# Rows of finished output units squared and scaled under the seventh unit, and the recurrence's additional turns gathered in one column group

## The chip, the cores and the metric

One core of a Trainium2 chip. The metric is the device time of one execution in microseconds, as the median of several runs; the kernel before took 1652.8 us (three runs, 1652.15 to 1653.36). Beside it stands one profiled execution, from which all rows of the profile come.

The engines are named as the profile names them: PE is TensorE (matmuls), PEld its weight loads, DVE is VectorE, ACT is ScalarE, POOL is GpSimd, SP is the engine whose queue issues most DMAs. Each engine works through its own instructions in the order that was fixed when the kernel was built.

## The reference

An encoder of two layers on a sequence of 512 rows with 2048 columns, all in float32. Layer 1 mixes grouped-query attention and a gated linear recurrence; layer 2 is a chunked mLSTM that runs forward and backward. Cut to what matters:

```python
# layer 1 (even)
proj = rmsnorm(x) @ w_in            # q, k, v, g_attn, x_lru, g_lru
attn = block_attention(rope(q), rope(k), v)                  # 8 heads, 2 key heads
xc = conv4(x_lru)
y = rg_lru(xc, ..., reverse=False) + rg_lru(xc, ..., reverse=True)
x = x + concat(attn * silu(g_attn), y * silu(g_lru)) @ w_out

# one direction of rg_lru: two gates, then a scan along the sequence
r = sigmoid(xb @ wa + ba); i = sigmoid(xb @ wx + bx)
a = exp(8 * r * log_sigmoid(lam)); u = sqrt(1 - a * a) * i * xc
h[t] = a[t] * h[t - 1] + u[t]

# layer 2 (odd)
q, k, v, o, z, gates = rmsnorm(x) @ w_in
h = mlstm(q, k, v, gates) + flip(mlstm(flip(q), ...))        # 8 heads
h = rmsnorm_per_head(sigmoid(o) * h) * silu(z)
x = x + h @ w_out

out = x * rsqrt(mean(x * x, axis=-1) + 1e-6) * final_gain
```

The last line matters most here: each row's factor needs the squares of all its 2048 columns.

## The kernel before, in words

**Layout.** The residual stream lies transposed: 128 columns of x on the partitions, 512 sequence rows along the free dimension. A pair of such column blocks is a unit of 256 columns: units 0 to 7 of the output. A weight product in float32 is made of three matmuls of rounded parts (high by high, low by high, high by low; `mm3`, L157), so every weight chunk is first split: ACT writes the high part (L153), DVE the rest (L154).

**Column groups and lanes.** `run_steps` works through a list of groups. An ordinary group makes 512 columns of a projection: eight steps c of a 256-deep weight chunk, in each four blocks b of six matmuls. The weights are loaded three steps ahead and split two steps ahead (`ahead`). Between the blocks other work is let in by turns: two lanes of Python generators, and `pump(lane)` runs the first generator of a lane up to its next `yield`. Lane 0 holds attention and, in layer 2, the heads; it gets a turn after block 1 of each step (`turns` names other blocks). Lane 1 holds the recurrent units of layer 1 and the transposes `hT_gen` of layer 2; it gets one turn at the end of each step, and additional ones where a group has `more`:

```python
if b == 1 and c % 8 < g.get("more", 0):
    self.pump(1)
```

In layer 1 the groups come in the order KV, Q0, L0, L1, Q1, GL0, GL1, GA0, GA1, and then four groups of the output product. L0 and L1 make the recurrence's input, and each adds two units `lru_gen` to lane 1. Such a unit has 13 turns: two convolutions with their splits (L862, L153, L154), four of gates (each six matmuls `lg` and two DVE additions, L880), one of sigmoid and tanh on ACT, one of exponentials and L912, one empty, one of square roots, one empty, and two of scans (L923, L925). The groups with `more=5` are Q1, GL0 and GL1. Lane 0 meanwhile does the first key head's attention up to Q1, the second one's q in GL0 and its attention from the end of GL0 to GA1. The output product's operands are made by `mix_split`, from step 0 of GA1 on; where a needed part isn't there, it draws the lanes dry. A finished part whose gate isn't there yet is stored to DRAM and loaded again (`value_ready`, `mix_load`).

In layer 2, `hT_gen` squares a head pair's result (L1183), works out the row factors, scales on ACT (L1194), and then transposes block by block on PE (`hT`).

**The output product.** Units 0 and 1 are one ordinary group; their rows are squared into the running sum `acc`, scaled, and stored to DRAM (`x3d`). Units 2 to 6 are made by seven products instead of eight (`run_w7`). Units 2 to 5 (`LATE`) are added in DRAM onto the residual `x2d` by an accumulating DMA from POOL's queue (`out2_onto`); unit 5's goes out in unit 6's fourth step. Unit 6 is added on the chip (`out2_7`, L1373), squared, scaled. During unit 6, a hook `each(c)` loads finished units back: 0, 1, 2, 3, 4 in steps 3 to 7; `run_last` loads what is missing, unit 5. All loads go by SP's queue, between the weight loads.

The slots that these rows need come from one pool of 37 (`NSLOT`), of which 32 hold the operands of the output product; unit 6 frees two a step.

**The last unit (`run_last`).** Unit 7 is made in three parts. `rows()` makes its columns for sequence rows 0 to 255; `columns(0)` and `columns(1)` make rows 256 to 383 and 384 to 511 with the roles of the operands exchanged. Ahead of them in the program stand the squares and scales of units 2 to 5: `late_square` for the halves h0 (sequence rows 0 to 255, sums on DVE) and h1 (256 to 511, sums on POOL), then `late_scale` for h0; `late_scale` for h1 comes after `rows()`. The addition of unit 7 (L1410) and its square (L1419) follow. The row sums `stc` (a matmul of `acc` and the last square with ones) are taken up at k = 1 of `columns(0)`; DVE works out the factors, PE spreads them (`rB`), and every row block is scaled (L1480) and stored.

**Order.** What each engine does in which order is planned at build time from program order and readiness: `high_priority` moves evacuations ahead, and an instruction that is planned to wait can be passed by later ones of the same engine. At run time nothing is passed.

Of the kernel before, what the change touches and what calls it, by code (L numbers as in the profile page):

```python
# [15 lines left out]
AF = mybir.ActivationFunctionType  # L16
ALU = mybir.AluOpType
# [15 lines left out]
LATE = (2, 3, 4, 5)  # L33
# [8 lines left out]
class Builder:  # L42
# [255 lines left out]
    def run_steps(self, groups):  # L298
        self.steps = [(g, c) for g in groups for c in range(NCH)]
        self.raw, self.wsp = {}, {}  # L300
        self.nload = self.nsplit = 0
        self.ahead(0, 2, 1)
        i = 0
        for g in groups:
            if g["lay"] == "W7":
                self.run_w7(g, i)
                i += NCH
                continue
            if g["lay"] == "W7c":
                self.run_w7c(g, i)  # L310
                i += NCH
                continue
            g["ps"] = [None] * 4
            while self.later:
                self.evac_later()
            if g["lay"] == "last":
                self.run_last(g, i)
                i += NCH
                continue
            for c in range(NCH):  # L320
                self.ahead(i, 3, 2)
                g["c"] = c
                ws = self.wsp.pop(i)
                for b in range(g.get("nb", 4)):
                    if c == 0:
                        g["ps"][b] = self.bank.tile([P, 512], F32, tag="bulk", name=self.name("bk"))
                    self.bulk_mm(g, g["ps"][b], g["x"](c), ws, b, c)
                    if (c < NCH - 1 or b < 1 and "turns" in g) and b in g.get("turns", (1,)):
                        self.pump(0)
                    if b == 1 and c % 8 < g.get("more", 0):  # L330
                        self.pump(1)
                    if c == NCH - 1 and b == 0 and g.get("mid"):
                        g["mid"]()
                if c == NCH - 1:
                    with self.tc.high_priority(offset=100):
                        for b in range(g.get("nb", 4)):
                            g["evac"](b, g["ps"][b])
                    if g.get("after"):
                        g["after"]()
                    self.pump(0)  # L340
                self.pump(1)
                i += 1
# [647 lines left out]
class Layer2(Layer1):  # L990
# [217 lines left out]
    def hT_gen(self, p):  # L1208
        nc = self.nc
        for hs in self.h_norm(p):  # L1210
            yield
        for c in (2 * p, 2 * p + 1):
            t = self.slot2("hT")
            if p < 3:
                z = [self.half("zt") for _ in range(2)]
                for j in range(2):
                    nc.sync.dma_start(out=z[j], in_=self.zTd[(2 * c + j) * P:(2 * c + j + 1) * P, :])
            for j in range(2):
                k = 2 * c + j
                f = slice((k - 4 * p) * P, (k - 4 * p + 1) * P)  # L1220
                ps = self.psum("hT")
                for tt in range(NT):
                    self.tr(ps[:, tt * P:(tt + 1) * P], hs[tt // 2][:, tt % 2, f], self.ident)
                gn = self.pb[:, PB_GN + k:PB_GN + k + 1]
                nc.scalar.activation(t[:, j, :], ps, AF.Copy, scale=gn)
                if p < 3:
                    nc.gpsimd.tensor_tensor(out=t[:, j, :], in0=t[:, j, :], in1=z[j], op=ALU.mult)
                yield
            if p == 3:
                self.h3[c] = t  # L1230
                continue
            nc.sync.dma_start(out=self.hTd[2 * c * P:(2 * c + 2) * P, :].rearrange("(j p) s -> p j s", p=P), in_=t)
            self.hT_stored.add(c)
# [148 lines left out]
        self.xres[i] = self.slot2("xres")  # L1382
        self.nc.sync.dma_start(out=self.xres[i], in_=self.x3d[i] if i in self.x3d else self.rows2(self.x2d, i))

    def late_square(self, i, cs):

        sq = self.half("sq3").rearrange("p (j s) -> p j s", j=2)
        self.nc.scalar.activation(sq, self.xres[i][:, :, cs], AF.Square)
        eng = self.nc.gpsimd if cs.start else self.nc.vector
        for j in range(2):  # L1390
            eng.tensor_tensor(out=self.acc[:, cs], in0=self.acc[:, cs], in1=sq[:, j, :], op=ALU.add)

    def late_scale(self, i, cs):
        for k in (2 * i, 2 * i + 1):
            x3 = self.xres[i][:, k % 2, cs]
            self.nc.scalar.activation(x3, x3, AF.Copy, scale=self.pb[:, PB_GF + k:PB_GF + k + 1])

    def out2_scale(self, k):
# [26 lines left out]
    def run_last(self, g, i0):  # L1425
# [104 lines left out]
                    nc.sync.dma_start(out=self.a["outc"][u * P:(u + 1) * P, :], in_=t)  # L1530
            yield

        h0, h1 = slice(0, 256), slice(256, 512)
        for cs in (h0, h1):
            for n in LATE:
                self.late_square(n, cs)
        for n in LATE:
            self.late_scale(n, h0)
        step = rows_norm(rows())
        for n in LATE:  # L1540
            self.late_scale(n, h1)
        step = columns_norm(0, *columns(0, step))
        for _ in columns_norm(1, *columns(1, step)):
            pass
# [2 lines left out]
    def build(self):  # L1547
# [14 lines left out]
        w1, wo1, w2, wo2 = a["even_w_in"], a["even_w_out"], a["odd_w_in"], a["odd_w_out"]  # L1562

        def grp(w, lo, lay, x, evac, **kw):
            return dict(w=w[:, lo:lo + 512], lay=lay, x=x, evac=evac, **kw)
# [15 lines left out]
        def hx(c):  # L1581
            return tuple(t.rearrange("p (t j) s -> p j t s", t=2) for t in self.hs[c]["B"])

        x1 = self.x1s.__getitem__
# [4 lines left out]
                      after=lambda: add(0, self.k_gen()))]  # L1589

        def after_q(g):
            def f():
                add(0, self.q_gen(g))
                add(0, self.attn_gen(g))
            return f
# [4 lines left out]
                add(1, self.lru_gen(2 * g + 1))  # L1600
            return f


        L = [grp(w1, 2560 + 512 * g, "T", x1, self.xlru_evac(g), after=after_lru(g)) for g in range(2)]
        Q = [grp(w1, 512 * g, "tok", x1, self.q_evac(g), after=after_q(g), more=5 * g) for g in range(2)]
        GA = [grp(w1, 1536 + 512 * g, "T", x1, self.gate_evac(2 * g)) for g in range(2)]
        GL = [grp(w1, 3584 + 512 * g, "T", x1, self.gate_evac(4 + 2 * g), more=5) for g in range(2)]
        groups += [Q[0], L[0], L[1], Q[1], GL[0], GL[1], GA[0], GA[1]]

        order = [0, 1, 4, 5, 6, 7, 2, 3]  # L1610
# [63 lines left out]
        def late2(c):  # L1674
            if c < NCH - 1:
# [2 lines left out]
        groups[-1]["pre"] = early2  # L1678
        groups.append(grp(wo2, 0, "T", hx, self.out2_evac, turns=TURNS, more=NCH,
                          pre=self.res_pre((0, 1), self.x2d, late2)))  # L1680
        def u7(i, evac, **kw):
            return dict(w=wo2[:, 256 * i:256 * i + 256], lay="W7", f=i + 1, order=range(NCH), x=self.hs.__getitem__,
                        evac=evac, **kw)

        groups += [u7(i, self.out2_onto(i)) for i in LATE]
        groups.append(u7(6, self.out2_7(6), pre=self.res_pre((6,), self.x2d),
                         each=lambda c: self.x3_load(c - 3) if c > 2 else None))
        groups.append(dict(w=wo2[:, 1792:2048], lay="last", order=range(NCH), pre=self.res_pre((7,), self.x2d)))
        self.run_steps(groups)

# [95 lines left out]
```

## Time and profile before

| | us |
|---|---|
| median of three runs | 1652.8 |
| the profiled execution | 1648.95 |
| its span | 1647.2 |
| PE busy | 1612.9 (98%) |
| DVE busy | 1125.2 (68%) |
| ACT busy | 847.3 (51%) |
| POOL busy | 754.4 (46%) |

The profiled execution's own time lies 1.75 us above its span and 3.85 us below the median of the runs. PE is counted as busy almost throughout; the stretches in which it isn't are few, and a view of the waits names them with the tile and the line that ended each. In the rows, `bk` and `s` are the sums of weight products in PSUM, `acc` the running sum of squares, `xres` a unit's rows, `lg` the recurrence's gates, `tr` a transpose, `stc` the row sums and `rB` the spread factors. The granted clock is given as a share of the full one.

### The profile page before, as it was taken

How to read it: one execution, taken by the hardware profiler on the slowest of the kernel's cores; microseconds unless marked ns; L12 is line 12 of the kernel's file. 1: busy time of each engine (PE TensorE's matmuls, PEld its weight loads, DVE VectorE, ACT ScalarE, POOL GpSimd, SP SyncE). 2: the span in 40 equal slices, each digit the busy share in tenths (PEclk: the TensorE clock that was granted, in tenths of full speed). 3: DMA queues.
4: the chain of work that ended last, by engine and by line, in shares of the span. 5: the costliest groups of instructions: out<-in, count | busy, mean ns of one | idle time of the engine just before them, and what ended most of it. 6: DMA issues, size and time to landing. Idle time of an engine off the chain costs nothing.

```text
span 1647.2 us, 25420 instructions
## 1 busy us (share of the span) xinstructions
PE 1612.9 (98%) x9698; PEld 1425.4 (87%) x9698; DVE 1125.2 (68%) x1714; ACT 847.3 (51%) x1400; POOL 754.4 (46%) x732
## 2 busy tenths in 40 slices
PE   9999999889999999999999999999999999999996
PEld 7888888678788888889999999999988888879996
DVE  8755487786554333457999986666776676688866
ACT  6334767478552333334444443444576566665434
POOL 5220225333000111386798778888511312468843
PEclk9999999999999999999999999999999999999997
DMA  7433131432343544644434443444654344443473
GB/s 231 134 96 91 52 116 64 128 97 69 94 137 116 179 167 162 195 134 129 128 118 140 129 142 116 129 129 129 205 171 131 109 154 154 156 151 103 129 228 108
DMA packets 139275, 220.23 MB, mean 134 GB/s; under 512 B 9856, under 2 KB 62464, under 8 KB 139152
## 3 DMA queue, kind: packets, MB, share of 16 engines
q1 hardware_dynamic: 136880, 215.90, 41.8%
q0 software_dynamic: 1088, 2.10, 0.8%
q8 instruction: 76, 1.25, 0.3%
q10 hardware_dynamic: 1184, 0.60, 0.1%
q14 instruction: 47, 0.39, 0.1%
HBM read 183.41 MB, written 35.16 MB: 133 GB/s over the span
## 4 chain that ended last, share of the span: by engine, by line
PE 81%; DVE 9%; ACT 4%; DMA 3%; issue 2%; POOL 2%; SPq 0%; DVEq 0%; ACTq 0%; POOLq 0%
PE bk L157 44%; PE s L157 28%; DVE wl L154 2%; PE nb L157 1%; PE nf L157 1%; PE lg L157 1%; PE ST L157 1%; POOL w7s L363 1%; PE PV L157 1%; PE S L157 1%; DMA x2d<-x 1%; PE tr L160 1%; DVE ltau L912 1%; DMA raw<-in_odd_w_out_dram 1%; DMA hTr<-hTd 1%
## 5 line engine op out<-in xcount | busy, mean ns | idle before, releaser
L154 DVE TENSOR_TENSOR wl<-raw,wh 128x1024 fp32r<-128x1024 f32 (+3 forms) x333 | 361.7, 1088 | 294.4 <-ACT wh L153 293.2
L153 ACT CAST wh<-raw 128x1024 fp32r<-128x1024 f32 (+3 forms) x333 | 265.9, 800 | 453.5 <-PE s L157 237.9
L363 POOL TENSOR_TENSOR w7s<-raw 128x256 f32<-128x256 f32 x216 | 226.7, 1069 | 91.8 <-DMA raw<-in_odd_w_in_dram 53.6
L154 DVE TENSOR_TENSOR wl<-w7s,wh 128x512 fp32r<-128x512 f32 (+1 forms) x176 | 203.6, 1157 | 5.3 <-ACT wh L153 5.3
L157 PE MATMUL s<-th,wl 128*128 128x256 f32 x544 | 153.0, 281 | 0.5 <-DVE wl L154 0.5
L157 PE MATMUL s<-tl,wh 128*128 128x256 f32 x544 | 152.8, 281 | 0.0
L157 PE MATMUL bk<-xh,wh 128*128 128x512 f32 x384 | 152.3, 397 | 0.4 <-DVE gate L809 0.4
L157 PE MATMUL s<-th,wh 128*128 128x256 f32 x544 | 152.7, 281 | 0.0
L157 PE MATMUL bk<-xl,wh 128*128 128x512 f32 x384 | 151.7, 395 | 0.0
L157 PE MATMUL bk<-xh,wl 128*128 128x512 f32 x384 | 151.4, 394 | 0.0
L153 ACT CAST wh<-w7s 128x512 fp32r<-128x512 f32 (+1 forms) x176 | 125.6, 714 | 13.4 <-POOL w7s L363 13.3
L363 POOL TENSOR_TENSOR w7s<-w7s,raw 128x256 f32<-128x256 f32 x108 | 116.2, 1076 | 0.0
L157 PE MATMUL s<-bh,wh 128*128 128x256 f32 x408 | 115.2, 282 | 0.0
L157 PE MATMUL s<-bh,wl 128*128 128x256 f32 x408 | 114.5, 281 | 0.2 <-DVE wl L154 0.2
L157 PE MATMUL s<-bl,wh 128*128 128x256 f32 x408 | 114.4, 280 | 0.0
L363 POOL TENSOR_TENSOR w7s<-raw,w7s 128x256 f32<-128x256 f32 x108 | 103.7, 960 | 7.8
L157 PEld LDWEIGHTS s<-th,wl 128*128 128x128 f32 x544 | 102.3, 188 | 0.7 <-DVE wl L154 0.7
L157 PEld LDWEIGHTS s<-th,wh 128*128 128x128 f32 x544 | 102.4, 188 | 0.0
L157 PEld LDWEIGHTS s<-tl,wh 128*128 128x128 f32 x544 | 102.4, 188 | 0.0
L157 PE MATMUL bk<-oh,wl 128*128 128x512 f32 x256 | 100.9, 394 | 0.0
L157 PE MATMUL bk<-ol,wh 128*128 128x512 f32 x256 | 100.8, 394 | 0.0
L157 PE MATMUL bk<-oh,wh 128*128 128x512 f32 x256 | 100.8, 394 | 0.0
(349 smaller groups left out, 4469.7 us busy)
## 6 DMA issues: line engine op xcount, KB each, us to landing
raw<-in_odd_w_in_dram SPq DMA_DIRECT2D x120, 512.0 KB, 3.9
raw<-in_even_w_in_dram SPq DMA_DIRECT2D x71, 512.0 KB, 3.7
raw<-in_even_w_out_dram SPq DMA_DIRECT2D x32, 512.0 KB, 3.6
raw<-in_odd_w_out_dram SPq DMA_DIRECT2D x32, 512.0 KB, 4.0
xres<-in_xT_dram SPq DMA_DIRECT2D x8, 512.0 KB, 6.0
x2d<-xres SPq DMA_DIRECT2D x8, 512.0 KB, 4.3
xgd<-xg SPq DMA_DIRECT2D x8, 512.0 KB, 4.3
xr<-xgd SPq DMA_DIRECT2D x8, 512.0 KB, 7.0
```

Of the source, the lines that this page charges most:

```text
L153: self.nc.scalar.copy(h, x)
L154: (eng or self.nc.vector).tensor_tensor(out=l, in0=x, in1=h.bitcast(F32), op=ALU.subtract)
L157: self.nc.tensor.matmul(out, a, b, start=start, stop=stop)
L160: self.nc.tensor.transpose(out, x, ident)
L363: po.tensor_tensor(out=s[:, :, q, :], in0=x, in1=y, op=op)
L912: v.scalar_tensor_tensor(out=tau[j][:, d, :], in0=e2, scalar=1.0, in1=tau[j][:, d, :], op0=ALU.add, op1=ALU.mult)
```

## The change

Three edits, and one that goes with them.

1. While unit 6 is made, units 2, 3 and 4 are loaded back in steps 2, 3 and 4 and unit 5 in step 7. In steps 5, 6 and 7 units 2, 3 and 4 are squared, summed into `acc` (half h0 on DVE, h1 on POOL, as before) and scaled, all 512 rows at once. `run_last` loads units 0 and 1, and squares and scales unit 5 only, ahead of `rows()`.
2. The additional turns of lane 1 (`more`) move from Q1, GL0 and GL1 (five each) to GA0 (eight). There they come after block 0 of each step instead of block 1; groups with `turns` keep block 1.
3. `hT_gen` has one more, empty, turn between the scaling and the first transposes.

```diff
-                    if b == 1 and c % 8 < g.get("more", 0):
+                    if b == (1 if "turns" in g else 0) and c < g.get("more", 0):
                         self.pump(1)
@@ hT_gen
         for hs in self.h_norm(p):
             yield
+        yield
         for c in (2 * p, 2 * p + 1):
@@
-    def late_square(self, i, cs):
-        sq = self.half("sq3").rearrange("p (j s) -> p j s", j=2)
-        self.nc.scalar.activation(sq, self.xres[i][:, :, cs], AF.Square)
-        eng = self.nc.gpsimd if cs.start else self.nc.vector
-        for j in range(2):
-            eng.tensor_tensor(out=self.acc[:, cs], in0=self.acc[:, cs], in1=sq[:, j, :], op=ALU.add)
-
-    def late_scale(self, i, cs):
+    def late_rows(self, i):
+        for h, eng in enumerate((self.nc.vector, self.nc.gpsimd)):
+            cs = slice(256 * h, 256 * h + 256)
+            sq = self.half("sq3").rearrange("p (j s) -> p j s", j=2)
+            self.nc.scalar.activation(sq, self.xres[i][:, :, cs], AF.Square)
+            for j in range(2):
+                eng.tensor_tensor(out=self.acc[:, cs], in0=self.acc[:, cs], in1=sq[:, j, :], op=ALU.add)
         for k in (2 * i, 2 * i + 1):
-            x3 = self.xres[i][:, k % 2, cs]
+            x3 = self.xres[i][:, k % 2, :]
             self.nc.scalar.activation(x3, x3, AF.Copy, scale=self.pb[:, PB_GF + k:PB_GF + k + 1])
@@ run_last
-        h0, h1 = slice(0, 256), slice(256, 512)
-        for cs in (h0, h1):
-            for n in LATE:
-                self.late_square(n, cs)
-        for n in LATE:
-            self.late_scale(n, h0)
+        self.late_rows(5)
         step = rows_norm(rows())
-        for n in LATE:
-            self.late_scale(n, h1)
         step = columns_norm(0, *columns(0, step))
@@ build, layer 1
-        Q = [grp(..., after=after_q(g), more=5 * g) for g in range(2)]
-        GA = [grp(w1, 1536 + 512 * g, "T", x1, self.gate_evac(2 * g)) for g in range(2)]
-        GL = [grp(w1, 3584 + 512 * g, "T", x1, self.gate_evac(4 + 2 * g), more=5) for g in range(2)]
+        Q = [grp(..., after=after_q(g)) for g in range(2)]
+        GA = [grp(w1, 1536 + 512 * g, "T", x1, self.gate_evac(2 * g), more=8 - 8 * g) for g in range(2)]
+        GL = [grp(w1, 3584 + 512 * g, "T", x1, self.gate_evac(4 + 2 * g)) for g in range(2)]
@@ build, output product
+        def late_rows(c):
+            if 2 <= c <= 4 or c == 7:
+                self.x3_load({2: 2, 3: 3, 4: 4, 7: 5}[c])
+            if c >= 5:
+                self.late_rows(c - 3)
+
         groups.append(u7(6, self.out2_7(6), pre=self.res_pre((6,), self.x2d),
-                         each=lambda c: self.x3_load(c - 3) if c > 2 else None))
+                         each=late_rows))
```

More of the change, by code (lines that the diff above doesn't have):

```diff
@@ L1604, in build @@
         L = [grp(w1, 2560 + 512 * g, "T", x1, self.xlru_evac(g), after=after_lru(g)) for g in range(2)]
-        Q = [grp(w1, 512 * g, "tok", x1, self.q_evac(g), after=after_q(g), more=5 * g) for g in range(2)]
-        GA = [grp(w1, 1536 + 512 * g, "T", x1, self.gate_evac(2 * g)) for g in range(2)]
-        GL = [grp(w1, 3584 + 512 * g, "T", x1, self.gate_evac(4 + 2 * g), more=5) for g in range(2)]
+        Q = [grp(w1, 512 * g, "tok", x1, self.q_evac(g), after=after_q(g)) for g in range(2)]
+        GA = [grp(w1, 1536 + 512 * g, "T", x1, self.gate_evac(2 * g), more=8 - 8 * g) for g in range(2)]
+        GL = [grp(w1, 3584 + 512 * g, "T", x1, self.gate_evac(4 + 2 * g)) for g in range(2)]
         groups += [Q[0], L[0], L[1], Q[1], GL[0], GL[1], GA[0], GA[1]]
```

## The prediction

> **What bounds the kernel now.** I read the page first, then TensorE's waits, then a table of windows, and last the timelines of the end.
>
> ```profile
> PE 1612.9 (98%) x9698; PEld 1425.4 (87%) x9698; DVE 1125.2 (68%) x1714; ACT 847.3 (51%) x1400; POOL 754.4 (46%) x732
> ```
>
> TensorE is busy for 1612.9 of 1647.2 us. Since the change takes no matmul away, all it can win lies in the other 34.3 us and in stretches at a low clock. The waits of TensorE (line that waited, what released it, total, times, longest) name the larger holes:
>
> ```profile
> PE lg L157 <- DVE qT L154: 6.1, 1, 6.1
> PE stc L157 <- DVE acc L1421: 5.5, 1, 5.5
> PE tr L160 <- ACT pm L793: 5.2, 2, 5.1
> PE rB L157 <- DVE diag L600: 2.8, 2, 2.6
> PE hT L160 <- ACT hfb L1194: 1.1, 3, 0.5
> ```
>
> The change touches three places: the end (stc), layer 1's column groups (lg and tr), and hT. The windows (columns: stretch, its length, then busy time of PE, PEld, DVE, ACT and POOL, granted clock, DMA share, GB/s) show where the layer-1 holes lie. I cut by the evacuations, so GL0, GL1 and GA0 are the first three rows, within a few us; the fourth is in the end.
>
> ```profile
> 277.00:337.00 60.00, 53.42 (x233) 42.77 (x232) 47.36 (x62) 31.49 (x41) 30.38 (x20) 0.94 0.35 114
> 337.00:403.00 66.00, 60.50 (x278) 49.30 (x278) 46.41 (x70) 49.38 (x71) 15.07 (x11) 0.97 0.29 88
> 403.00:461.00 58.00, 56.21 (x283) 46.68 (x282) 35.59 (x51) 33.72 (x52) 8.03 (x4) 1.00 0.36 109
> 1620.00:1630.00 10.00, 8.14 (x37) 8.01 (x38) 3.67 (x19) 4.84 (x14) 2.87 (x4) 0.52 0.01 2
> ```
>
> TensorE idles 6.6, 5.5 and 1.8 us in the three groups, 13.9 in sum. The clock's deficit is 0.06 x 60 + 0.03 x 66 = 5.6 us; part of it falls inside the idle time, so I count half, 2.8. At stake in layer 1: 16.7 us.
>
> **Part 1, the rows of units 2 to 5 at the end.** Timelines of ACT, DVE, POOL and PE (start, duration, engine, line, operation, tiles, count, idle before); the row with x440 is one of the chain that ended last and gives the pace of a 256-wide matmul, 52.13 / 440 = 0.118 us:
>
> ```profile
> 1613.50 4.26 ACT L1388 ACTIVATE sq<-xres 128x512 f32<-128x512 f32 x8
> 1617.67 3.29 ACT L1396 ACTIVATE xres<-xres,pb 128x256 f32<-128x256 f32 x8
> 1620.86 0.70 ACT L1419 ACTIVATE sq<-xres 128x256 f32<-128x256 f32 x2
> 1611.86 2.66 POOL L1421 TENSOR_TENSOR acc<-acc,sq 128x512 f32<-128x512 f32 x2 [23.44 <-ACT sq L1419]
> 1616.35 6.76 POOL L1391 TENSOR_TENSOR acc<-acc,sq 128x256 f32<-128x256 f32 x8 [1.83 <-ACT sq L1388]
> 1614.55 5.40 DVE L1391 TENSOR_TENSOR acc<-acc,sq 128x256 f32<-128x256 f32 x8 [2.85 <-POOL acc L1421]
> 1619.88 0.74 DVE L1410 TENSOR_TENSOR xres<-xres,bk 128x256 f32<-128x256 f32 x2
> 1621.29 0.42 DVE L1421 TENSOR_TENSOR acc<-acc,sq 128x256 f32<-128x256 f32 x1 [0.68 <-ACT sq L1419]
> 1502.26 52.13 PE s L157 x440
> 1601.58 0.28 PE L157 MATMUL bk<-bh,wh 128*128 128x256 f32 x1
> 1613.26 0.61 PE L157 MATMUL bk<-ident,xres 128*128 128x128 f32 x4
> 1621.86 0.56 PE L157 MATMUL stc<-ones,acc 128*128 128x2 f32 x2 [5.51 <-DVE acc L1421]
> 1624.13 0.41 PE L157 MATMUL bk<-wh,bl 128*128 128x256 f32 x1
> 1628.82 0.99 PE L157 MATMUL rB<-diag,ones 128*128 128x256 f32 x2
> 1629.65 0.28 PE L157 MATMUL stc<-ones,acc 128*128 128x2 f32 x2
> ```
>
> The row sums (stc) need acc, and in front of it stand eight adds on DVE (5.40) and 7.5 us of squares and scales on ACT, so that unit 7's two squares come only at 1620.86. Afterwards three of four units are squared and scaled under unit 6; two adds (5.40 / 8 = 0.68 each) remain. They start when POOL is through unit 6's two (1611.86 + 2.66 = 1614.5): 1614.5 + 1.35 (adds) + 0.74 (L1410) + 0.2 (what of its squares isn't beside the second addition) + 0.42 (last add) = 1617.2. That is 4.65 us earlier than 1621.86.
>
> Where on TensorE's queue the sums then stand I can't read from this trace. They are written before the second of sixteen k-steps of columns(0), but stood behind the eighth; the order is fixed when the kernel is built, and with inputs planned early they may move up to 1613.6. If they stay, the wait is 0.9 us; if they move to the front, 3.6. The work is the same, but with 3.6 us the k-steps come afterwards. From 1617.2 in that case: 1.1 us of sums (4 x 0.28), 45 matmuls at 0.118 = 5.3, the spread 0.5 and the 0.15 behind it, hence columns(1) starts at 1624.3 instead of 1629.8 (1629.65 and the sums there): **5.5 us won**. If they stay at the eighth, the DVE chain from the sums to diag binds. I have no single row for it; it took less than the 7.0 us from 1621.86 to 1628.82, and thirteen small instructions and two wider ones on DVE make 3.2 of it at about 0.2 each. 1617.2 + 1.1 + 3.2 + 0.5 = 1622.0 instead of 1629.65, or 7.65 won. The low end: before, the hole of 5.51 us was followed by half clock (0.41 us a matmul, window row 0.52) up to between the 0.99 of 1628.82 and the 0.28 of 1629.65, some 7.4 us, worth 3.7. Should a hole of 3.6 also bring that on, 5.5 - 3.7 = 1.8 is left. I take 5.5, as the sums are written in front; range 1.8 to 7.65. The 17.4 us from 1629.8 to the end I leave alone.
>
> The trace agrees with the Trainium skill (page "TensorE: Matmul & The Clock Gate", section "What's actually happening"): an idle window of about 3.4 us halves the clock, the window running freely, until a busy window. By it a 3.6 us hole may fall on either side, so the page gives 1.8 or 5.5 here; the holes in this trace of 5.5 (dropped) and 1.8 (GA0's clock stays 1.00) leave it open too.
>
> **What hides the moved work.** DMA and split rows of the last stretch:
>
> ```profile
> 1585.68 0.81 SPq L1383 DMA_DIRECT2D xres<-x3d  x2
> 1597.75 0.36 SPq L1383 DMA_DIRECT2D xres<-x2d  x1
> SPq L1383 <- DMA x2d<-x: 6.6, 1, 6.6
> xres<-x2d SPq DMA_DIRECT2D x5, 512.0 KB, 10.4
> 1604.73 1.05 ACT L153 CAST wh<-raw 128x1024 fp32r<-128x1024 f32 x1 [4.53 <-DMA raw<-in_odd_w_out_dram]
> 1600.24 1.23 DVE L154 TENSOR_TENSOR wl<-raw,wh 128x1024 fp32r<-128x1024 f32 x1 [3.71 <-ACT wh L153]
> 1605.81 1.23 DVE L154 TENSOR_TENSOR wl<-raw,wh 128x1024 fp32r<-128x1024 f32 x1 [4.35 <-ACT wh L153]
> ```
>
> Eight 512 KB reads (units 0 to 7) are issued either way; only the order differs. Units 2, 3 and 4 now take the place of 0 and 1 from 1585.7 on; at 10.4 us to land they are there by 1597. ACT's share per unit is two squares (4.26 / 8 = 0.53) and two scales twice as wide as L1396's 0.41, at most 2.7 us, 8.1 in all; 4.5 us of that fit into the hole before 1604.73 alone, and DVE's holes behind ACT (3.71, 4.35) show that ACT had as much room before the cast ahead of it. Unit 5's load still waits for its own accumulating write, as unit 4's did for the slot of that write (SP's 6.6 us); behind both wait the last two weight loads. With one read fewer ahead of the write this could come earlier; I count 0. The last splits are tight: that of 1605.81 ends at 1607.0, and TensorE needs it at 1601.6 + 48 x 0.118 = 1607.3. A cover that fails costs up to 2.7 us there, one unit's share of ACT; this is the other end, and lies inside the range of the end.
>
> Against putting adds on POOL and DVE at one time speaks the Trainium skill (page "SBUF — State Buffer", section "SBUF: two separate sides"): a GpSimd instruction locks out a DVE one with two SBUF inputs. The trace agrees, 0.68 against 0.42 us for the same add; by the rule six POOL adds of 0.85 could hold DVE for 5.1 us, which fits into the three holes before its splits, so the sum stands by both.
>
> **Part 2, the turns.** One unit of recurrence takes 13 turns of lane 1. Before, groups Q1, GL0 and GL1 give 13 turns each and GA0 the last four. Afterwards Q1, GL0 and GL1 give 8, GA0 16, and the last three fall in GA1. DVE's price is a quarter of these rows a unit:
>
> ```profile
> L862 DVE SCALAR_TENSOR_TENSOR xc<-xpad,pb,xc 128x512 f32<-128x512 f32 x24 | 17.5, 764 | 0.0
> L912 DVE SCALAR_TENSOR_TENSOR ltau<-le,ltau 128x512 f32<-128x512 f32 x16 | 16.6, 1074 | 10.4 <-POOL le L911 10.4
> L925 DVE TENSOR_TENSOR_SCAN ltau<-lr,li 128x512 f32<-128x512 f32 x8 | 12.2, 1530 | 0.0
> L880 DVE TENSOR_SCALAR lr<-lg,pb 128x512 f32<-128x512 f32 x16 | 12.0, 747 | 15.5 <-PE lg L157 15.5
> L880 DVE TENSOR_SCALAR li<-lg,pb 128x512 f32<-128x512 f32 x16 | 12.0, 747 | 0.0
> L923 DVE TENSOR_TENSOR_SCAN ltau<-lr,li 128x512 f32<-128x512 f32 x8 | 11.9, 1483 | 0.0
> L154 DVE TENSOR_TENSOR lws<-lwr,lws 128x512 fp32r<-128x512 f32 x8 | 5.5, 686 | 1.3 <-ACT lws L153 1.3
> L154 DVE TENSOR_TENSOR xchl<-xc,xchl 128x512 fp32r<-128x512 f32 x8 | 5.5, 686 | 0.7 <-ACT xchl L153 0.7
> ```
>
> Convolution and splits 7.1, gates 6.0, L912 4.1, scans 6.0: 23.3 us. GL0 loses a whole unit and gets two gate turns, one L912 and half the scans (10.1): DVE from 47.4 to 34.2 us. GL1 loses a unit too and gets half the scans, two convolutions with splits and four gate turns (16.1): 46.4 to 39.2. GA0: 35.6 + 21.4 = 57 us in about 62 (its 58, less the hole of 1.8, plus 24 gate matmuls of twice 0.118). GL0's wait was for DVE: busy 47.4 of 53.4 us outside the hole, 89%. At 64% it should go. GL1's wait came as gates, roots and attention met at its start; two thirds of that should go, as the recurrence is then at its scans. GA0 becomes what GL0 was, 92%, and I charge it GL0's price, 6.6 + 1.5 of clock = 8.1. Left in GL1 about 1.6. Sum: 16.7 - 8.1 - 1.6 = **7 won**; bounds 16.7 won (no hole) and 6.3 lost (rival d).
>
> **Part 3, the empty turn.** It puts a stretch of matmuls between the scaling and the transposes: 0 to 1.1 us (hT's waits). Two turns of the last unit are then drawn in one go by h_split. I take **0.5**, with 0.5 lost as the other end.
>
> Sum against the profiled execution (1648.95, its span 1647.2): 1648.95 - 5.5 - 7 - 0.5 = 1636. The median of the runs is 1652.8, 3.85 higher: **1640 us**.
>
> **Rivals.** (a) GA0's hole grows until layer 1 wins nothing: 57 of 62 us of DVE, and attention in the same lanes. Against it: its neighbour GA1 is light. 5.5 + 0.5 won: 1647. (b) Both places give all: 16.7 + 7.65 + 0.5: 1628. GL0's 64% speaks for it, GA0's 92% against. (c) The change doesn't do what it says at the end: the sums move to the front, the hole keeps the clock at half, 1.8 is left, layer 1 as in (a): about 1651. (d) Slower: GA0 stalls twice. Both convolution turns of unit 3 fall in one step of it, its sigmoid and exponential turns in another. A step has 24 bulk matmuls, 24 x 0.236 = 5.7 us; DVE's 7.1 for two convolution turns and 1.2 for the weight split exceed that before attention has had its part, and the next weight split stands behind them. At GL0's price twice (16.2), with GL1's hole left as it is (5.5 and 1.3 of clock), layer 1 goes from 16.7 to 23, 6.3 lost; the end wins only its 1.8: 1657. It decides from where a burst's backlog exceeds attention's lead, two steps of 62 / 8, 15.5 us. For it speaks the 92%, against it that GL1, with two turns in five of its steps before, had no hole past its start.
>
> **Numbers.** Forecast 0.46 (own range 1634 to 1646), (a) 0.24, (b) 0.08, (c) 0.12, (d) 0.10. Below 1630 and above 1650 lies about a fifth, hence 1630 to 1650. A difference under 0.2%, 3.3 us, can't be told from none: (c) is mostly within. Faster 0.81, same 0.09, slower 0.10.
>
> **What would show it.** After: the sixteen 256-wide scales of L1396 gone, one pair of adds on DVE behind unit 6; stc's wait 1 to 3.6 us; rB about 7 us earlier against the last unit's start; lg's wait on qT gone; DVE near 90% in GA0. Wrong, if TensorE's idle time between 277 and 520 us is not below 10, or if stc's wait is above 4.

## The result: 9.5 us in the first runs, 5.5 in a second set

The changed kernel took 1643.0 us (median of four runs, 1641.33 to 1645.47) beside 1652.5 for the kernel before: a ratio of 0.9943 (95% interval 0.9926 to 0.9961). A second set of runs, five of the changed kernel beside nine of the one before, gave 1646.0 against 1651.5, ratio 0.9964 (0.9951 to 0.9976). So the change is faster, by 0.4 to 0.6%. Its own runs spread over 5 us; part of the reason is one of the findings.

The profiled execution of the first set took 1641.33 us, span 1639.6. The page's line of busy times:

```profile
PE 1610.4 (98%) x9698; PEld 1424.1 (87%) x9698; DVE 1122.1 (68%) x1714; ACT 850.1 (52%) x1395; POOL 745.6 (45%) x732
```

Those of TensorE's waits that bear on the change (what waited, for what; total, times, longest):

```profile
PE bk L157 <- DVE wl L154: 6.4, 2, 5.7
PE PV L157 <- DVE ptl L154: 2.9, 2, 2.7
PE rB L157 <- DVE diag L600: 2.3, 2, 2.2
PE s L157 <- ACT wh L153: 1.7, 3, 0.9
PE s L157 <- DVE wl L154: 1.1, 3, 0.5
PE tr L160 <- ACT pm L793: 1.0, 1, 1.0
PE nb L157 <- ACT hT L1226: 0.9, 1, 0.9
PE stc L157 <- DVE acc L1421: 0.9, 1, 0.9
```

The wait of `lg` (6.1) is gone, tr's fell from 5.2 to 1.0 and stc's from 5.5 to 0.9. New are one of 5.7 us for a weight split (`wl`), 2.7 for `ptl`, and smaller ones at `s` and `nb`, where there were nearly none. The windows of layer 1, cut at the same times as before (stretch, length, busy time of PE, PEld, DVE, ACT and POOL, granted clock, DMA share, GB/s); the last row, 461 to 516, lies almost wholly in GA1:

```profile
277.00:337.00 60.00, 60.00 (x272) 48.85 (x271) 44.31 (x61) 40.18 (x49) 20.71 (x14) 1.00 0.34 101
337.00:403.00 66.00, 65.75 (x325) 54.53 (x324) 37.34 (x63) 47.14 (x72) 11.37 (x9) 1.00 0.21 60
403.00:461.00 58.00, 54.33 (x260) 44.62 (x259) 42.25 (x59) 42.17 (x60) 14.40 (x11) 0.97 0.29 91
461.00:516.00 55.00, 48.30 (x204) 39.05 (x203) 35.10 (x32) 27.63 (x32) 10.06 (x5) 0.91 0.39 133
```

The holes of GL0 and GL1 (6.6 and 5.5 us) are closed; GA0 idles 3.7 us instead of 1.8, and the window of GA1, which had no idle time and full clock before, idles 6.7 us at a clock of 0.91. Idle in sum: 10.6 us, against 13.9. The groups themselves end earlier here: the last gate evacuation of GL0 starts at 323.81 instead of 342.05, GL1's at 384.49 instead of 410.68, GA0's at 457.40 instead of 467.75. So each of the first three windows also holds the start of the next group.

The end of the changed kernel (timelines of PE, ACT and DVE: start, duration, operation, idle before):

```profile
1602.34 0.28 PE L157 MATMUL bk<-bh,wh 128*128 128x256 f32 x1
1603.31 1.05 ACT L153 CAST wh<-raw 128x1024 fp32r<-128x1024 f32 x1 [0.57 <-DMA raw<-in_odd_w_out_dram]
1604.26 0.58 ACT L487 COPY w7u<-s 128x512 f32<-128x512 f32 x1
1608.99 1.28 DVE L1374 TENSOR_TENSOR xres<-xres,x 128x512 f32<-128x512 f32 x2
1613.18 1.30 DVE L1393 TENSOR_TENSOR acc<-acc,sq 128x256 f32<-128x256 f32 x2 [2.91 <-POOL acc L1421]
1614.41 0.74 DVE L1410 TENSOR_TENSOR xres<-xres,bk 128x256 f32<-128x256 f32 x2
1615.35 0.42 DVE L1421 TENSOR_TENSOR acc<-acc,sq 128x256 f32<-128x256 f32 x1 [0.20 <-ACT sq L1419]
1615.92 0.35 PE L157 MATMUL stc<-ones,acc 128*128 128x2 f32 x2 [0.89 <-DVE acc L1421]
1620.08 0.70 PE L157 MATMUL rB<-diag,ones 128*128 128x256 f32 x2 [0.18 <-DVE diag L600]
```

One pair of adds (1.30) stands where eight (5.40) stood. From unit 7's first matmul to the row sums it takes 13.6 us instead of 20.3, and to the end of the span 37.3 instead of 45.6.

**Where the 7.6 us between the two profiled executions lie.** Milestones, in us of each span:

| milestone | before | after | won up to here |
|---|---|---|---|
| last gate evacuation of GA1 starts | 515.87 | 513.68 | 2.2 |
| first `nb` on `wB` | 1208.7 | 1207.3 | 1.4 |
| last `nb` | 1446.5 | 1446.3 | 0.2 |
| unit 2's first matmul | 1502.5 | 1500.2 | 2.3 |
| unit 7's first matmul | 1601.6 | 1602.3 | -0.7 |
| end of the span | 1647.2 | 1639.6 | 7.6 |

Layer 1 gave 2.2 us, the end 8.3; 0.8 were lost between layer 1 and the heads, the heads lost 1.2, the transposes won 2.1, and units 2 to 6 lost 3.0 of it again. These are differences of two single executions, and that of the kernel before (1648.95) lies 3.5 us under the median of its set. The experiments take them apart.

### The profile page after: what moved, and what is told of

Read it like the earlier page. It is cut to its first block, busy times and chain, and to the rows that moved or that the text cites. A ratio compares the mean times of both kernels' runs of the same rounds, so it can differ in the third digit from the quotient of the medians.

```text
span 1639.6 us, 25389 instructions
## 1 busy us (share of the span) xinstructions
PE 1610.4 (98%) x9698; PEld 1424.1 (87%) x9698; DVE 1122.1 (68%) x1714; ACT 850.1 (52%) x1395; POOL 745.6 (45%) x732
## 4 chain that ended last, share of the span: by engine, by line
PE 83%; DVE 6%; ACT 4%; POOL 3%; issue 3%; DMA 1%; SPq 0%; DVEq 0%; POOLq 0%; ACTq 0%
PE bk L157 44%; PE s L157 29%; DVE wl L154 2%; PE nb L157 2%; PE nf L157 1%; PE PV L157 1%; PE ST L157 1%; PE lg L157 1%; PE S L157 1%; PE tr L160 1%; ACT wh L153 1%; PE gt L157 0%; DMA hTr<-hTd 0%; DVE ltau L923 0%; DVE ltau L925 0%
## 5 line engine op out<-in xcount | busy, mean ns | idle before, releaser
L363 POOL TENSOR_TENSOR w7s<-raw 128x256 f32<-128x256 f32 x216 | 222.5, 1048 | 95.5 <-DMA raw<-in_odd_w_in_dram 68.2
L363 POOL TENSOR_TENSOR w7s<-w7s,raw 128x256 f32<-128x256 f32 x108 | 120.3, 1114 | 0.0
L903 POOL TENSOR_TENSOR li<-li,xc 128x512 f32<-128x512 f32 x16 | 21.4, 1361 | 191.9 <-ACT li L895 191.9
L363 POOL TENSOR_TENSOR w7s<-raw,w7s 128x256 f32<-128x256 f32 x108 | 101.1, 936 | 7.8
```

The source lines that it names most:

```text
L363: po.tensor_tensor(out=s[:, :, q, :], in0=x, in1=y, op=op)
L903: nc.gpsimd.tensor_tensor(out=ii[j][:, d, :], in0=ii[j][:, d, :], in1=xc[:, j, :], op=ALU.mult)
```

## The experiments

Each is given with its ratio to the kernel before in the same set of runs and the 95% interval.

**1. The moved rows alone.** The kernel before, `late_square` and `late_scale` replaced by `late_rows`; turns and transposes as before.

```diff
-        for cs in (h0, h1):
-            for n in LATE:
-                self.late_square(n, cs)
...
+        self.late_rows(5)
```

> The kernel before with the moved rows alone (turns and empty turn as before). Theory A, read from the two profiles (unit 7 start to span end 45.6 us before, 37.2 after): the end gains 8.4 us however the rest runs, so 1652.5 - 8.4 = about 1644, and columns(1) starts about 19.2 us behind unit 7's start, the wait before stc is under 1.5 us. Theory B, the prediction's term: 5.5 us, about 1647, the rest of the 8.4 having come from the state in which the other two edits leave POOL and ACT at the end. If B holds, the wait before stc is 3 to 4 us and TensorE keeps half speed after it.

Measured: 1647.0 us, 0.9968 (0.9956 to 0.9980), 5.3 us won. By time theory B, and its sign was there too, if smaller: stc waited 2.63 us, and TensorE then ran at half clock for 6.8 us. But B's reason was wrong: not POOL or ACT at the end, but a transfer. In every kernel profiled with the moved rows and the weight loads as they were, the row sums follow the cast of unit 7's third weight block at the same distance, and only that cast moves:

| kernel | cast of block 3 behind unit 7's start | sums behind that cast | wait of stc | unit 7's start to the end |
|---|---|---|---|---|
| before | 3.1 | 17.1 | 5.5 | 45.6 |
| changed, first profile | 1.0 | 12.6 | 0.9 | 37.3 |
| rows alone (1) | 2.7 | 12.6 | 2.6 | 41.9 |
| no empty turn (4) | 3.2 | 12.6 | 3.1 | 42.5 |
| changed, second profile (5) | 2.6 | 12.6 | 2.5 | 39.9 |
| five turns in GL1 (8) | 3.6 | 12.6 | 3.4 | 42.6 |
| three turns in GL1 (10) | 2.8 | 12.6 | 2.7 | 40.0 |
| a multiplication on DVE (11) | 2.1 | 12.6 | 2.0 | 39.5 |

The chain became 4.5 us shorter in all seven; in 2 and 3, without the moved rows, it is 17.1 as before. What stands at its head is a weight block: ACT casts it in front of unit 6's evacuation (L487), so the evacuation, the squares of unit 6, POOL's adds and the sums all wait for the block to land. Its load stands on SP's queue right behind a load of residual rows: in the changed kernel's first profile that load is issued at 1597.86 and the block's at 1598.32. In these profiles the block is issued 2.5 to 4.0 us ahead of unit 7's start and is cast 5.0 to 6.5 us after its issue.

**2. The moved turns alone.**

```diff
+                    if b == (1 if "turns" in g else 0) and c < g.get("more", 0):
...
+        Q = [grp(..., after=after_q(g)) ...]
+        GA = [grp(..., self.gate_evac(2 * g), more=8 - 8 * g) ...]
+        GL = [grp(..., self.gate_evac(4 + 2 * g)) ...]
```

> The kernel before with the moved turns alone. Theory A: layer 1 gains 2.2 us at its last gate evacuation as in the changed kernel (515.9 to 513.7 us), which reaches the end nearly whole: 1650 to 1651. Theory B: the gain of layer 1 is swallowed at unit 2, where the POOL work behind the reloaded hT rows ends at the same absolute time whatever came before: 1652 to 1653, and TensorE waits about 2 us more between 1490 and 1520. The prediction's term (7 us, 1645.5) would need the hole in GA1 to come from elsewhere: idle in 461:516 below 3 us.

Measured: 1648.8 us, 0.9978 (0.9968 to 0.9987), 3.6 us won. Below both theories, and B is refuted: no idle time at all between 1500 and 1520. GA1 idles 6.7 us here as well, so the hole belongs to this edit. The last gate evacuation starts only 0.7 us earlier than before; in this execution GA0's window is at a clock of 0.94. Over all profiles it starts at 515.9 to 516.9 with the turns as before (before, 1, 3) and at 513.3 to 515.2 with them moved as here (changed, 2, 4 to 7): about 2 us apart. The end took 44.4 us instead of 45.6, with half clock for 6.8 us (until about 1627.2) where it lasted 10.2 before; that part is the clock's doing, not the turns'. Where the rest of the 3.6 us comes from, one profile doesn't show: its execution took 1649.14 us, the profiled one of the kernel before 1648.95.

**3. The empty turn alone.**

```diff
         for hs in self.h_norm(p):
             yield
+        yield
```

> The kernel before with the empty turn alone. The prediction's term: 0.5 us won, 1652.0. Rival, read from the profiles: the later hT rows cost about 2 us at unit 2 and win 1 at the waits for hT, so about 1 us lost: 1653.5.

Measured: 1655.0 us, 1.0016 (1.0005 to 1.0027): 2.6 us lost. The rows of the matmuls `s<-th,wh` of units 2 to 6 (count, shortest/median/longest, first and last start) and of the last head pair's sums on POOL, first of the kernel before:

```profile
L157 PE MATMUL s<-th,wh x160: 274/281/285, 1502.5 to 1601.2; 128*128 128x256 f32 x160
1480.48 1.72 POOL L549 TENSOR_TENSOR ts<-hT 128x256 f32<-128x256 f32 x1
1506.06 1.10 POOL L363 TENSOR_TENSOR w7s<-raw,w7s 128x256 f32<-128x256 f32 x1
```

then of the empty turn alone, with its wait at the heads:

```profile
PE nb L157 <- ACT hT L1226: 0.9, 1, 0.9
L157 PE MATMUL s<-th,wh x160: 277/280/415, 1504.8 to 1607.4; 128*128 128x256 f32 x160
1485.21 1.66 POOL L549 TENSOR_TENSOR ts<-hT 128x256 f32<-128x256 f32 x1 [1.16 <-DVE hT L1346]
1510.75 1.10 POOL L363 TENSOR_TENSOR w7s<-raw,w7s 128x256 f32<-128x256 f32 x1
```

From the first to the last such matmul, unit 2 to unit 6, it takes 102.6 us instead of 98.7. POOL works through one chain without a pause: sums (`ts`) of the last head pair's product, then unit 2's weight sums (`w7s`), 25.6 us between the two rows shown in either kernel. With the empty turn POOL idles 1.16 us for the pair's product (`hT`; no idle time before), and counted from the last `nb` its row comes 0.4 us later, while TensorE, spared its waits at the transposes, reaches unit 2 earlier by 2.0. The last of those weight sums starts 3.6 us behind unit 2's first matmul before, 5.9 with the empty turn, and TensorE waits there for splits of unit 2's weights (`wh`, `wl`). In this execution the clock then fell to half for 3.4 us (granted clock 0.66 between 1515 and 1520), which costs 1.7; in both profiles of the changed kernel it stayed full there. The wait of `nb` for `hT` is new as well. The rival is borne out, at 2.6 us instead of 1.

**4. The changed kernel without the empty turn.** The same line taken out of the changed kernel.

> The changed kernel without the empty turn (rows and turns as changed). The prediction's term: 0.5 us slower than the changed kernel, 1643.5. Rival, that the empty turn delays what POOL does ahead of unit 2: about 1 to 2 us faster than the changed kernel, 1641 to 1642, with the 2 us of TensorE waits between 1500 and 1510 gone.

Measured: 1644.6 us, 0.9955 (0.9943 to 0.9967). The waits between 1500 and 1520 are gone, as the rival said, and units 2 to 6 take 99.1 us from start to unit 7 again (102.2 and 101.1 in two profiles of the changed kernel); but the third weight block came 3.2 us behind unit 7's start here, and the end took 42.5 us. From the times alone nothing could be concluded; 7, below, decides it.

**5. The changed kernel again.**

> The changed kernel itself once more. Theory A: its end depends on when the third weight block of unit 7 lands, which differs from run to run (0.9 us behind unit 7's start in the changed kernel's first profile, 2.7 and 3.2 in the two other kernels with moved rows, which also kept half clock behind stc). The runs then spread over some 4 to 5 us, 1641 to 1646, and the profile shows either a landing near 1 us with a wait before stc of about 0.9, or one near 3 us with a wait of 2.5 to 3 and sums at 352 ns instead of 251. Theory B: the empty turn makes the difference: the landing is again near 1 us and the wait before stc 0.9, all runs 1641 to 1643.

Measured: 1646.0 us (1643.12 to 1646.55), 0.9964 (0.9951 to 0.9976). Theory A, with a landing between its two values. The end of its profile (ACT, then PE; then two windows: stretch, length, PE busy, granted clock, DMA share, GB/s):

```profile
1604.01 1.05 ACT L153 CAST wh<-raw 128x1024 fp32r<-128x1024 f32 x1 [1.66 <-DMA raw<-in_odd_w_out_dram]
1616.61 0.35 PE L157 MATMUL stc<-ones,acc 128*128 128x2 f32 x2 [2.55 <-DVE acc L1421]
1617.98 0.42 PE L157 MATMUL bk<-wh,bh 128*128 128x256 f32 x1
1616.00:1618.00 2.00, 1.40 (x12) 0.96 0.00 0
1618.00:1620.00 2.00, 2.00 (x11) 0.50 0.00 0
```

The sums and the matmuls up to 1617.9 ran at full clock; then, with TensorE at work again for 1.2 us, the clock fell to half for 3.4 us. B falls: the empty turn is in this kernel, and the block still landed 2.6 us behind unit 7's start. So the 0.9 us of wait in the first profile was a lucky draw: in the seven profiles of the table with the moved rows the wait runs from 0.9 to 3.4 us and the end from 37.3 to 42.6.

**6. Unit 7's third and fourth weight block loaded early.** The changed kernel; the two blocks go into free slots of the row pool, from unit 6's last two steps on, the third ahead of unit 5's reload on SP's queue.

```diff
-        raw = self.wp.tile([P, 2, 512], F32, tag="raw", ...)
+        raw = self.slot2("raw") if g["lay"] == "last" and c >= 4 else self.wp.tile([P, 2, 512], F32, tag="raw", ...)
@@ late_rows(c), the hook of unit 6
+            self.ahead(len(self.steps) - 16 + c, 6 if c >= 6 else 4, 0)
```

> The changed kernel; the third and fourth weight block of unit 7 are loaded into free slots of the row pool, the third from unit 6's seventh step, ahead of unit 5's reload in SP's queue. Theory A (the end waits for that landing: cast of the third block, unit 6's evacuation, its squares, POOL's adds): unit 6's evacuation follows its last matmul at once, the wait before stc is 1 us or less in every run, full clock behind it, and unit 7's start to the end takes 36.5 to 37.5 us: about 1640, and the runs spread less. Rival, that POOL's adds and ACT's squares bind the end whatever lands when: no more than 1 us from the changed kernel beside it.

Measured: 1643.5 us (1641.17 to 1644.63), 0.9949 (0.9936 to 0.9963), 2.5 us less than the changed kernel beside it, though the two sets of times overlap.

```profile
1605.34 1.04 ACT L153 CAST wh<-raw 128x1024 fp32r<-128x1024 f32 x1
```

The cast of block 3 no longer waits for a transfer (it starts 0.9 us behind unit 7's start, with no idle time before it), the sums come 13.6 us behind that start without a wait, at full clock, and the end took 38.0 us. Theory A, except that the time is 3.5 us above the forecast and the end 0.5 above its range: I had started from the lucky profile of the changed kernel. The runs spread as widely as the changed kernel's (3.5 us against 3.4), against theory A, so the landing is not all that moves them. What bears the cause out is the end: in the four profiles with early weight blocks (6, 7, 9, 12) it takes 37.1 to 38.0 us, and `stc` has no wait.

**7. The same without the empty turn.**

> The kernel with the early weight blocks, without the empty turn. Theory A (the empty turn costs 2 to 2.5 us: 1.2 at the products of the last heads, 3 at the start of unit 2, less 2 won at the transposes): 2 to 2.5 us faster than the kernel with the early weight blocks, about 1637.5 to 1638. Rival (the empty turn is worth 0.5 us or makes up at the end what it costs): not faster.

Measured: 1639.9 us (1639.31 to 1641.09), 0.9933 (0.9921 to 0.9945), 3.6 us less than 6 in the same set. With the landing out of the way, the empty turn's price shows: it is not worth 0.5 us, it costs 3.6 here and 2.6 alone (3).

**8. Five additional turns in GL1 too.** The changed kernel, one argument more:

```diff
-        GL = [grp(..., self.gate_evac(4 + 2 * g)) for g in range(2)]
+        GL = [grp(..., self.gate_evac(4 + 2 * g), more=5 * g) for g in range(2)]
```

> The changed kernel with five additional turns of the recurrence in GL1 too, so that the last unit ends in step 6 of GA0 instead of step 3 of GA1. Theory A (the 5.7 us hole in GA1 comes from unit 3's scans and splits meeting there with the attention's and mix splits): it goes, idle in 461:516 below 2 us, 4 to 7 us won, if GL1 and GA0 stay as they are. Rival: the load was only moved; idle time of the same size opens in 337:403 or 403:461, and the time is that of the changed kernel within 2 us.

Measured: 1633.0 us (1631.68 to 1634.23), 0.9889 (0.9876 to 0.9903): 13 us less than the changed kernel beside it, by a change of five turns. Its windows:

```profile
277.00:337.00 60.00, 60.00 (x271) 48.89 (x270) 48.17 (x67) 41.88 (x53) 20.73 (x14) 1.00 0.35 106
337.00:403.00 66.00, 65.02 (x321) 53.64 (x320) 47.25 (x71) 54.36 (x78) 18.62 (x12) 1.00 0.22 65
403.00:461.00 58.00, 57.41 (x279) 46.95 (x278) 43.41 (x57) 46.35 (x64) 17.88 (x12) 1.00 0.31 94
461.00:516.00 55.00, 54.59 (x243) 44.45 (x243) 25.51 (x25) 19.20 (x22) 0.00 (x0) 1.00 0.45 146
```

2.0 us of idle time are left in layer 1, at full clock everywhere, although GL1 carries ten us more of DVE than in the changed kernel (47.25 against 37.34). The last gate evacuation starts at 500.87: 15.0 us earlier than in the kernel before, nearly all of the 16.7 us that were at stake. Theory A, and more than it gave.

**9. All three together:** five turns in GL1, early weight blocks, no empty turn.

> The changed kernel with all that the runs so far point to: five turns in GL1 (12 to 13 us won beside the changed kernel), the early weight blocks of unit 7 (about 2.5), no empty turn (about 3). If the three gains add, 1627 to 1629; TensorE idle in 277:516 at about 2 us, the sums full speed behind a wait under 1 us. Rival: what is won in layer 1 is partly lost again at later places that wait for POOL and for DMA, as in the turns-only kernel: 1630 to 1633.

Measured: 1626.65 us (1626.31 to 1627.97), 0.9845 (0.9831 to 0.9859). The gains add. The largest of its waits, and its sums (PE), which stand without one:

```profile
PE rB L157 <- DVE diag L600: 2.4, 2, 2.2
PE hT L160 <- ACT hfb L1194: 1.1, 3, 0.5
PE s L157 <- DVE wl L154: 1.1, 3, 0.5
PE bk L157 <- DVE wl L154: 1.0, 2, 0.7
1600.65 0.35 PE L157 MATMUL stc<-ones,acc 128*128 128x2 f32 x2
```

This kernel beats the one before by 25 us and the changed one by 16 to 19.

**10. Three turns in GL1 instead of five.** `more=3 * g` in the line of 8: the recurrence ends in GA0's last step.

> The changed kernel with three additional turns in GL1 instead of five: the last unit of the recurrence then ends in the last step of GA0. Theory A (a threshold: what costs is that the last unit's exponentials, roots and scans fall among GA0's gates and GA1's first splits): a good part of the hole comes back, 3 to 8 us of the 12.5, 1637 to 1641, with idle between 455 and 480. Theory B (what costs is only turns in GA1): no turn is left in GA1, so all of the gain stays, 1633 to 1634.

Measured: 1634.95 us (1633.61 to 1639.09), 0.9896 (0.9880 to 0.9912). Near theory B: layer 1 idles 4.4 us between 277 and 516 instead of 2.0, so a little comes back, but no hole. (Its profiled execution is the one of 1639.09, which also lost clock at unit 2's start, 0.83 between 1500 and 1520; the median is what counts.) What costs is a turn of the recurrence in GA1, or something that only those turns bring with them.

**11. One multiplication on DVE instead of POOL.** The changed kernel; turns as changed, so three of them still fall in GA1.

```diff
-                nc.gpsimd.tensor_tensor(out=ii[j], in0=ii[j], in1=tau[j], op=ALU.mult)     # L918
+                (v if i == 3 else nc.gpsimd).tensor_tensor(out=ii[j], in0=ii[j], in1=tau[j], op=ALU.mult)
```

> The changed kernel, the multiplication ahead of the last unit's scans (L918) on DVE instead of POOL. Theory A (the scan at the head of DVE's queue waits for POOL's two multiplications, 4.74 us, and the weight split stands behind it): the scans start about 2 to 3 us earlier, the 5.7 us wait for wl in GA1 shrinks to 2 to 4 us, 2 to 4 us won. Rival (table loads on ACT, six between 450 and 465, make the roots late): the hole stays above 5 us and the time is that of the changed kernel within 1 us.

Measured: 1633.9 us (1632.51 to 1636.2), 0.9891 (0.9876 to 0.9907). The hole in GA1, row by row, in the changed kernel (POOL, DVE, ACT, PE):

```profile
466.55 4.74 POOL L918 TENSOR_TENSOR li<-li,ltau 128x1024 f32<-128x1024 f32 x2 [2.01 <-ACT ltau L917]
464.57 0.69 DVE L912 SCALAR_TENSOR_TENSOR ltau<-le,ltau 128x512 f32<-128x512 f32 x1
468.98 3.39 DVE L923 TENSOR_TENSOR_SCAN ltau<-lr,li 128x512 f32<-128x512 f32 x1 [3.72 <-POOL li L918]
472.29 1.19 DVE L925 TENSOR_TENSOR_SCAN ltau<-lr,li 128x512 f32<-128x512 f32 x1
473.41 1.19 DVE L154 TENSOR_TENSOR ol<-mixr,oh 128x1024 fp32r<-128x1024 f32 x1
474.52 2.28 DVE L154 TENSOR_TENSOR wl<-raw,wh 128x1024 fp32r<-128x1024 f32 x1
468.26 1.04 ACT L153 CAST wh<-raw 128x1024 fp32r<-128x1024 f32 x1
476.86 0.80 PE L157 MATMUL bk<-xh,wl 128*128 128x512 f32 x1 [5.71 <-DVE wl L154]
```

and with the multiplication on DVE (DVE, then the window of GA1):

```profile
466.46 2.36 DVE L918 TENSOR_TENSOR li<-li,ltau 128x1024 f32<-128x1024 f32 x2 [1.24 <-ACT ltau L917]
469.88 1.22 DVE L154 TENSOR_TENSOR wl<-raw,wh 128x1024 fp32r<-128x1024 f32 x1
473.88 1.22 DVE L923 TENSOR_TENSOR_SCAN ltau<-lr,li 128x512 f32<-128x512 f32 x1
461.00:516.00 55.00, 54.01 (x240) 43.68 (x239) 39.28 (x37) 29.62 (x34) 6.34 (x3) 1.00 0.46 152
```

In the changed kernel the last unit's scan stands at the head of DVE's queue. It waits 3.7 us for POOL's first multiplication, runs beside the second one for 3.39 us, and the weight split whose high part was cast by 469.3 starts at 474.52. TensorE stands still for 5.71 us and then runs below full clock. With the two multiplications on DVE (1.2 us each instead of 2.4 on POOL) the split runs at 469.88, 4.6 us earlier, and the order on DVE is another: the scan comes after it. Idle in GA1 falls from 6.7 to 1.0 us, the clock stays full. Theory A, with about three times the gain that it named; the table loads on ACT, the rival, were left in place, so they are not what makes the hole. Nor is it DVE's load: DVE has 2.4 us more to do here. The edit takes away the wait for POOL and changes DVE's order at once, so the shares of the two are not separated. In the profiles the last gate evacuation starts 8.3 us earlier than in the changed kernel's first (505.41 against 513.68); for the rest of the 12 us between the medians no run separates a cause.

**12. The empty turn for the first three head pairs only,** on the kernel of 9.

```diff
+        if p < 3: yield
```

> The kernel with all three edits that won, with the empty turn back, but for the first three head pairs only. Theory A (the empty turn of the last head pair is what costs: its transposes' products reach DVE and POOL later, and unit 2's first splits wait behind POOL's sums): no wait at unit 2's start, so 98.5 to 99.5 us from unit 2's first matmul to unit 7's, and only the 1 us at the products of the last heads (nb for hT) comes: 0.5 to 1.5 us slower than without any empty turn, 1627 to 1628. Rival (any empty turn delays the reloaded hT rows, the last pair's or the earlier ones', and so POOL's sums): unit 2 to unit 7 takes 101 us or more and the time is 1629 or more.

Measured: 1627.5 us (1627.45 to 1627.64), 0.9851 (0.9837 to 0.9864), 0.9 us above 9, with times that overlap those of 9. The time is theory A's, but the stretch from unit 2's to unit 7's first matmul is 100.2 us, between the two theories (99.1 in 9). So the last pair's turn is the larger part of the price, and the other pairs' has a part of about 1 us there too, beside the 1.2 us at the heads.

## Why the prediction was right, and where it was not

1640.0 was forecast, 1630 to 1650, faster at 0.81; 1643.0 and 1646.0 came. The direction holds, and so does the range. That the range holds says little: it would also have held with parts 2 and 3 at nothing (1647), and of these two one was wrong in size and one in sign. The three edits alone add up to 5.3 + 3.6 - 2.6 = 6.3 us, near the second set; the first set is nearer to the forecast by a lucky end. By steps:

- **What bounds the kernel:** right. No gain came from anywhere but TensorE's idle time and its clock.
- **Part 1, the end (5.5 won, 1.8 to 7.65).** The term was right, 5.3 alone. "4.65 us earlier" for the sums was the best step: the chain is 4.5 us shorter in every profile. The position was right, too: `stc` stands behind the second k-step, nearly in front, as chosen. The two cases "with half clock" and "without" were both real, but holes of 2.0 to 2.7 us were enough for half clock, and the profile from which the wait was worked out had a random part in it that I took as fixed: the landing of the weight block (the row of 1604.73 with its 4.53 us was quoted, as spare room for ACT, not as the head of the chain). The end won between 3.0 and 8.3 us from one profile to the next, more than the range allowed above.
- **What hides the moved work (0):** right as a price. ACT's rows under unit 6 delayed splits (the cast of unit 7's first block starts 7.4 us ahead of unit 7 before, 3.5 in 1), but from unit 2's to unit 7's first matmul it takes 99.4 us in 1 and 99.1 in 4, and 99.1 before. The last splits, called tight, were near the place that mattered: not the split of the third block, but unit 6's evacuation behind its cast.
- **Part 2, the turns (7 won).** This step failed, by size: layer 1 gave 2.2 us in the changed kernel, 0.7 in 2. The holes of GL0 and GL1 closed as forecast. GA0 did not become what was forecast, 57 us of DVE in about 62, or 92%: from GL1's last gate evacuation to GA0's it took 72.9 us with 50.3 of DVE, 69%, and TensorE idled 3.9 us in it. In the same way GL1 had 36.9 us of DVE in 60.7 (39.2 forecast); GL0's fixed window has 44.3 (34.2 forecast), but its last 13 us are GL1. What failed is the price put at nothing: the last three turns were seen to fall in GA1, and GA1 was dismissed as light. It holds no slack for a stall, because its weight splits and mix splits stand in the same queue as the last unit's scan. The price there (6.7 us idle, a clock of 0.91 over 55 us) has the form of rival (d), a burst in front of a weight split, one group later than put, and not by DVE's load but by DVE waiting for POOL. Rival (b), "all given", was 8% likely; 8 shows that its 16.7 us in layer 1 were nearly there, one line away (15.0).
- **Part 3, the empty turn (0.5 won, 0.5 lost at worst).** Wrong in sign: 2.6 lost alone. The 1.1 us at the transposes were won as written, and more (2.0 from the last `nb` to unit 2). The step that failed is "two turns of the last unit are then drawn in one go by h_split": I saw that the work behind it moves, and put no price on POOL's chain behind the last head pair, which ends where unit 2 begins: unit 2's first matmul to unit 7's took 3.8 us more in 3, and the heads 1.2.
- **What would show it.** L1396's 256-wide scales, the pair of adds and the wait of `lg` behaved as said; rB came 9.5 us earlier against unit 7's start instead of 7 (6.7 in the second profile). The mark "idle time below 10 us between 277 and 520" was missed, at 10.6, and it was the right mark for part 2. "DVE near 90% in GA0" was missed as well, at 69%.

The sum was off by 3 to 6 us: some 4 to 5 us in part 2, 3 in part 3, against which the first profile set a lucky end.

## What to carry to other kernels

Before a term is built on a wait, look at what stands at the head of its chain: if it is a transfer, the profile shows one draw of several, and loading earlier can win what a shorter chain leaves. Moving work by turns moves its tail too: follow the last operation of the moved chain to the queue in which it will stand, and look for another engine's result that it waits for there, since every split behind it waits as well. And a stage in which the engine is light can still be the worst place for a burst, if the bound engine's operands are made in that queue.

## What the runs showed of the hardware

- **A short hole can cost half clock after it has ended.** Holes of 2.0 us (11), 2.5 (5), 2.7 (10) and 3.4 (8) in front of the narrow row sums brought TensorE to half clock; the hole of 0.9 did not. In these four the clock fell 3.7 to 5.0 us after the hole began, when TensorE was working again; in 2 and 4 it fell inside the hole, 2.4 to 2.5 us after its start. The slow stretch lasted 3.4 us in 5, 10 and 11, 6.8 in 1, 2, 3, 4 and 8, and 10.2 at the end of the kernel before and around the hole in GA1 of the changed kernel. So the same 2 to 3 us of waiting cost 1.7 us more in one execution and 3.4 in another. The Trainium skill (page "TensorE: Matmul & The Clock Gate", section "What's actually happening") puts it down to an activity window of 3413 ns that runs freely; the stretches of one, two and three times 3.4 us agree with that. That a hole of 2.0 us is enough, the page does not say; whether the sums of two columns each that follow it count as little activity, no run here separates.
- **A scan beside a POOL operation.** The scan of 3.39 us in the changed kernel ended 1.1 us after POOL's second multiplication (466.55 + 4.74 = 471.29; 468.98 + 3.39 = 472.37); the same scan without POOL beside it takes 1.2 (11). So it seems to have stood still until POOL was through. The Trainium skill (page "SBUF — State Buffer", section "SBUF: two separate sides") says that a DVE operation with two SBUF inputs and a GpSimd one lock each other out for a whole instruction; the trace agrees.
- **The same multiplication of 128x1024 takes 1.2 us on DVE and 2.4 on POOL**: two took 2.36 us in 11 and 4.74 in the changed kernel.
